# Output projection of a hybrid encoder layer: operands as scaled fp16 pieces, y split where it arises

## The chip, the cores and the metric

The kernel runs on one core of a Trainium2 chip. Each engine (TensorE "PE", VectorE "DVE", ScalarE "ACT", GpSimd "POOL", SyncE "SP") takes its own queue of instructions in order; DMAs are issued from SP's queue. The metric is the device time of one execution in microseconds, the median of the runs. Lower is better.

## The reference

One layer on x of 1024 tokens by 1024 features, in float32. Eight heads of group A attend in a sliding window with ALiBi and learned sinks, eight of group B to their own chunk and eight chunks before it with a learned bias. Each group's output is normalised over its 512 columns with a gain of its own; both together go through one output projection, and the result is added to x. An MLP with squared ReLU follows.

```python
n = rms_norm(x, g)
q, k, v = split(n @ w_in)                       # columns of groups A and B
ya = rms_norm(mixer_a(qa, ka, va, sinks), ga)   # 512 columns
yb = rms_norm(mixer_b(qb, kb, vb, rel_bias), gb)
h = x + concat(ya, yb) @ w_out                  # the part that is changed
out = rms_norm(h + relu(rms_norm(h) @ w1) ** 2 @ w2)
```

## The kernel before

Tokens stand in 8 blocks of 128 (tb), or 2 halves of 512 (t). Heads go in pairs of 128 columns: A0 to A3 are m = 0 to 3, B0 to B3 are m = 4 to 7. Attention runs in units, A0_0 to A3_6 and then B0_0 to B7_1 (a head of B and a half): scores S, softmax rows P, transposes pt copied to T_A (group A; ACT L630, DVE L177) or transposed by DMA to G_B (group B), and products with V in PSUM "av". Between the pieces of a unit, a Filler places steps of the input projections (PSUM ip_qA1, ip_vB3 and so on) and later the steps of the first half of the output projection, out_proj_a (PSUM op_A, tag "w", two banks, which the input projections share). out_proj_b (op_B) follows after the last unit, at the start of the MLP part.

Every large product is made of pieces: mm3 (L200) issues y0*w0, y0*w1 and y1*w0, where index 0 is an operand rounded to a narrower type and 1 what is left of it. In the output projection the pieces are fp32r, 4 bytes each. out_proj_step makes one such triple for a pair q, a token block tb and a half of the columns; 8 blocks by 2 halves by 4 pairs by 3 products are 192 matmuls of 128x512 for each of op_A and op_B.

What makes the operands:

- **y of group A.** UnitA.apply (L800, L801) adds up the two halves of PSUM into Y; Pair.finish (L678 on) stores Y to DRAM (ya, 8 x 256 KB). load_ya brings it back ahead of op_A (four for t = 0, four for t = 1), and split_ya splits it with the norm's gain ogc: a copy on ACT (L914), the rest on DVE (L917). SPLIT_FIRST and SPLIT_AT say in which steps.
- **y of group B.** finish splits Y directly, with the gain and V's scale in one factor (V[2]); m = 4 to 6 go out to yd and come back (load_y, 512 KB a half), m = 7 stays.
- **w_out.** out_weight loads 128 rows into st_o, copies on ACT (L228) and subtracts on POOL (L177, 32 of 128x256).
- **norms.** squares of Y are added up in sqA and sqB; group_rstd turns them with 16 one-column matmuls (ss_A, ss_B) into rows of tokens; ACT (L1064) multiplies op_A by it while it empties PSUM, and residual (L1242) does so for op_B.

The order: matmuls keep the program's order (pe, "program order"). The other engines' queues, SP's among them, are put in order by a scheduler before the run; each engine then waits at the head of its queue. Tiles come from pools with tags: "pg" (33 pages), "ws" (three staging tiles of 4 KB a partition, in which st_kB, st_qB, st_vB and st_o land), "tst". A DMA into a tile can only be issued when its last reader is done.

## Time and profile before

| | us |
|---|---|
| median of 3 runs | 1041.23 (1040.61 to 1041.39) |
| the profiled execution | 1040.53 |
| its span | 1038.7 |
| TensorE busy | 1000.8 |
| op_A, 192 matmuls | 58.0 |
| op_B, 192 matmuls | 46.8 |

The span runs from the first instruction to the last; some 1.8 us of the execution lie around it. "Busy" for matmuls counts overlapping time: a mean duration of 428 or 396 ns (op_A, op_B) is longer than the distance from one start to the next, so the pace is read from unbroken runs in the chain of waits. A row of the timeline has start, duration, engine, line and operation, and in brackets how long the engine was idle before it and what ended that.

### The profile page before, as it was taken

What the parts mean: (1) busy time and instruction counts of PE and PEld (TensorE: products, weight loads), DVE (VectorE), ACT (ScalarE), POOL (GpSimd) and SP (SyncE); (2) the same over time, 40 slices, a digit from 0 to 9 for tenths busy, and PEclk for the clock granted to TensorE, in tenths of its full rate; (3) what the DMA queues carried; (4) which work ended last, traced back from release to release, by engine and by line L of the source; (5) the groups of instructions that cost most, each with busy time, mean ns of one, the idle gap of its engine ahead of it and who ended that gap; (6) DMA issues with size and microseconds to landing.
All of it is one profiled execution on the core that took longest, in us unless ns stands there. A gap on an engine that the chain in (4) does not pass through costs nothing.

```text
span 1038.7 us, 14057 instructions
## 1 busy us (share of the span) xinstructions
PE 1000.8 (96%) x4818; PEld 591.8 (57%) x4818; DVE 742.5 (71%) x1259; ACT 692.6 (67%) x1102; POOL 443.9 (43%) x341
## 2 busy tenths in 40 slices
...
PEclk9999999999989999989999999999999999999999
...
GB/s 353 254 133 133 129 82 184 194 209 225 209 257 251 207 261 182 62 21 166 211 282 293 205 210 274 195 170 310 257 329 388 189 150 186 159 121 122 1 1 162
DMA packets 150567, 200.63 MB, mean 193 GB/s; under 512 B 78688, under 2 KB 96224, under 8 KB 150496
## 3 DMA queue, kind: packets, MB, share of 16 engines
...
q8 instruction: 38, 0.62, 0.3%
...
## 4 chain that ended last, share of the span: by engine, by line
PE 34%; ACT 8%; issue 7%; DMA 7%; DVE 6%; POOL 2%; SPq 1%; DVEq 0%; POOLq 0%; ACTq 0%
PE f_a L171 13%; PE f_c L171 7%; PE f L171 6%; PE f_b L171 4%; DMA w<-in_w_ff_dram 3%; PE op_B L171 2%; ACT w L1362 2%; DMA m<-in_w_ff_dram 2%; DMA u<-ud 2%; POOL W L1397 2%; ACT k L1459 1%; ACT k L1458 1%; ACT W L1395 1%; DMA G_B<-H_B 1%; ACT m L1176 1%
## 5 line engine op out<-in xcount | busy, mean ns | idle before, releaser
L171 PE MATMUL f<-X,W 128*128 128x512 f16 x1344 | 295.3, 381 | 6.6 <-POOL W L1397 5.0
L171 PEld LDWEIGHTS <-U 128*128 128x128 f16 x1356 | 133.0, 98 | 163.9 <-issue 7.2
L171 PEld LDWEIGHTS <-W 128*128 128x128 f16 x1344 | 131.4, 98 | 166.3 <-POOL W L1397 8.2
L1397 POOL TENSOR_TENSOR U<-u,U 128x1024 f16<-128x1024 f32 x48 | 117.3, 2454 | 170.5 <-ACT U L1395 155.2
L171 PE MATMUL f_a<-V,U 128*128 128x512 f16 x756 | 165.3, 379 | 1.0 <-DVE C L1711 1.0
L1397 POOL TENSOR_TENSOR W<-T,W 128x1024 f16<-128x1024 f32 x29 | 69.7, 2407 | 84.3 <-ACT W L1395 84.3
L1397 POOL TENSOR_TENSOR W<-w,W 128x1024 f16<-128x1024 f32 x21 | 51.6, 2458 | 98.6 <-ACT W L1395 98.6
L171 PE MATMUL f_c<-V,U 128*128 128x512 f16 x384 | 86.0, 384 | 3.5 <-DVE V L1399 2.2
L1393 ACT ACTIVATE u<-u,uup 128x1024 f32<-128x1024 f32 x48 | 53.9, 1141 | 53.1 <-DMA u<-ud 53.0
L1399 DVE SCALAR_TENSOR_TENSOR V<-Z,up,V 128x1024 f16<-128x1024 f32 x32 | 51.3, 1605 | 28.7 <-ACT V L1395 20.7
L1395 ACT ACTIVATE U<-u 128x1024 f16<-128x1024 f32 x48 | 50.2, 1046 | 28.1 <-DVE Z L1369 10.4
L623 ACT ACTIVATE P_B<-P_B,nm_B 128x640 f32<-128x640 f32 (+2 forms) x64 | 44.2, 691 | 32.2 <-DVE nm_B L620 16.6
L171 PE MATMUL op_A<-w_o,y 128*128 128x512 f32 x192 | 58.0, 428 | 4.1 <-DVE ts_vB L433 3.9
L868 DVE SCALAR_TENSOR_TENSOR H_B<-P_B,rc_B,H_B 128x640 f16<-128x640 f32 (+2 forms) x64 | 51.0, 825 | 13.6 <-ACT H_B L863 13.3
L1399 DVE SCALAR_TENSOR_TENSOR V<-w,up,V 128x1024 f16<-128x1024 f32 x24 | 42.2, 1756 | 18.0 <-ACT V L1395 13.8
L171 PE MATMUL ip_qB<-nT,w_qB 128*128 128x512 f32 x192 | 53.7, 406 | 1.1 <-DVE t_kB L407 1.0
L171 PE MATMUL ip_kB<-nT,w_kB 128*128 128x512 f32 x192 | 53.7, 405 | 0.0
L1457 DVE CUSTOM_DVE_ANT_0 k<-f,k 128x1024 f32<-128x1024 f32 x24 | 29.3, 1220 | 31.3 <-PE f L171 22.4
L171 PE MATMUL ip_vB<-nT,w_vB 128*128 128x512 f32 x192 | 51.3, 400 | 0.0
L1395 ACT ACTIVATE V<-Z,up 128x1024 f16<-128x1024 f32 x32 | 36.4, 1138 | 22.2 <-DVE Z L1369 19.3
L171 PE MATMUL ip_qA<-nT,w_qA 128*128 128x512 f32 x192 | 50.7, 398 | 0.3 <-DVE VA L177 0.3
L863 ACT ACTIVATE H_B<-P_B,rc_B 128x640 f16<-128x640 f32 (+2 forms) x64 | 40.8, 685 | 9.5 <-DVE rc_B L860 4.2
...
## 6 DMA issues: line engine op xcount, KB each, us to landing
w<-in_w_ff_dram SPq DMA_DIRECT2D x64, 512.0 KB, 7.5
u<-ud SPq DMA_DIRECT2D x56, 512.0 KB, 5.4
ud<-k SPq DMA_DIRECT2D x48, 512.0 KB, 3.1
m<-in_w_ff_dram SPq DMA_DIRECT2D x32, 512.0 KB, 5.8
...
xr<-in_x_dram SPq DMA_DIRECT2D x8, 512.0 KB, 8.8
st_o<-in_w_out_dram SPq DMA_DIRECT2D x8, 512.0 KB, 4.8
h<-in_x_dram SPq DMA_DIRECT2D x8, 512.0 KB, 4.9
```

Source lines behind the costliest of these rows:

```text
L171: pe(nc.tensor.matmul(*args, **kw))
L623: nc.scalar.activation(pr, pr, AF.Exp, bias=nm, scale=-1.0, accum_out=sm)
L863: nc.scalar.activation(hi, q, AF.Copy, scale=rc)
L868: nc.vector.scalar_tensor_tensor(lo, q, rc, hi, ALU.mult, ALU.subtract)
L1176: nc.scalar.activation(src, src, AF.Square, accum_out=self.column())
L1362: nc.scalar.activation(w, w, AF.Copy, scale=up1)
L1393: nc.scalar.activation(full, full, AF.Copy, scale=up)
L1395: nc.scalar.activation(w[0], full, AF.Copy, scale=1.0 if up is None else up)
L1397: engine.tensor_tensor(w[1], full, w[0], ALU.subtract)
L1399: engine.scalar_tensor_tensor(w[1], full, up, w[0], ALU.mult, ALU.subtract)
L1457: dve.tensor_tensor_reduce(v, ps, v, 1.0, 0.0, ALU.add, ALU.max, top)
L1458: nc.scalar.activation(v, v, AF.Relu, scale=down1[n])
```

## The change

- **Scale of group A's y.** While V of group A is made, DVE takes the largest magnitude of each half (topA). scale_of_y turns it into powers of two: upA, by which Y is scaled as it leaves PSUM (ACT's copy and DVE's addition, now a SCALAR_TENSOR_TENSOR), dnA and dnA2, by which the norm undoes it. Group B's V is scaled already; its Y gets 2^-14.
- **Split where it arises.** finish splits every Y into two fp16 pieces (copy on ACT, subtraction on POOL, on DVE for the last one). Pairs 0 to 5 go to yd (two DMAs of 256 KB each) and come back as one of 512 KB; pairs 6 and 7 stay. ya, split_ya, split_y and their places are gone.
- **Weights.** The gain goes into w_out. A power of two per group is taken from a bound of its rows: bound_weights loads each of the eight 128-row blocks once more (bo0 to bo7, staging tag "ws") in the units 2 to 9, and the unit after squares it on ACT with a running sum. scale_of_weights makes the scale per group at B2_0 and at B7_0, each with one 128x128 transpose on TensorE (all_o0, all_o1) and some ten small DVE operations. out_weight then copies with that factor on ACT and takes the rest on DVE; POOL has no part in it any more.
- **Undoing.** rA is multiplied by dnA and owdn, rB by owdn.
- PAD, an unused strip of memory, grows from 32 to 40, and one small tile moves to another pool.

```diff
-SPLIT_FIRST = {(1, 1, 2): 0, (1, 1, 5): 1}
-SPLIT_AT = {(0, 0): (2, 0), (0, 2): (3, 0), (2, 1): (0, 1), (2, 3): (1, 1), (2, 5): (2, 1), (2, 7): (3, 1)}
...
+Y_UP, Y_DOWN, O_UP = 13, 14, 12
+BOUND_AT = 2
+SPREAD_B = "B7_0"
+PAD = 40
...
+    yd = dram([6, P, 2, 2, HALF], "yd", F16)
...
+    def root_of_bits(e):
+        i = e.bitcast(I32)
+        nc.vector.tensor_scalar(i, i, float(1 << 23), 0.5, ALU.add, ALU.mult)
+        nc.vector.tensor_scalar(i, i, 0xFF << 23, None, ALU.bitwise_and)
+        nc.vector.tensor_scalar(i, i, 1.0, float(63 << 23), ALU.mult, ALU.add)
+        return e
...
+    def bits_over(cols, name, psum, tag, bufs, least):
+        top = scale_tile("gtop", name, 2)
+        nc.vector.tensor_reduce(top, cols, mybir.AxisListType.X, ALU.max)
+        spread = psum.tile([P, P], F32, tag=tag, bufs=bufs, name=f"all_{name}")
+        transpose(spread, top.to_broadcast([P, P]), ident)
+        top = scale_tile("gall", name, 2)
+        nc.vector.tensor_reduce(top, spread, mybir.AxisListType.X, ALU.max)
+        return bits_of(top, name, least)
...
             nc.vector.tensor_tensor(f(st[:, 0]), acc, R1[:, c], ALU.mult)
+            nc.vector.tensor_reduce(
+                topA[:, t : t + 1], f(st[:, 0]), mybir.AxisListType.X, ALU.max, apply_absolute_value=True
+            )
...
-                for k, _ in enumerate(in_proj(*a, wa, (t,))):
-                    if (t, i, k) in SPLIT_FIRST:
-                        split_ya(SPLIT_FIRST[t, i, k], 0)
-                    yield
+            for a, wa in zip((q, v), w):
+                yield from in_proj(*a, wa, (t,))
...
-            if self.kind == "A":
-                nc.sync.dma_start(ya[self.m, :, t], Y)
-            elif self.y is None:
-                y = page([P, 2, HALF], f"y{t}_{self.m}")
-                low = split_y(y, Y, self.V[2], by_act)
-                def rest():
-                    if by_act:
-                        low()
-                    nc.sync.dma_start(yd[self.m - 4, :, t], f(y))
-                if by_act:
-                    late.append(rest)
-                else:
-                    rest()
+            if self.y is None:
+                y = page([P, 2, HALF], f"y{t}_{self.m}", F16)
             else:
-                self.y.append(page([P, 2, HALF], f"y{t}_{self.m}"))
-                split_y(self.y[t], Y, self.V[2])
+                if t == 0:
+                    self.y.append(page([P, 2, 2, HALF], f"y_{self.m}", F16))
+                y = self.y[0][:, t]
+            nc.scalar.activation(y[:, 0], Y, AF.Copy)
+            low = nc.vector if (self.m, t) == (7, 1) else nc.gpsimd
+            low.tensor_tensor(y[:, 1], Y, y[:, 0], ALU.subtract)
+            if self.y is None:
+                nc.sync.dma_start(yd[self.m, :, t], y)
...
-                nc.scalar.activation(y, self.av[HD:, :, s, :], AF.Copy)
-                nc.vector.tensor_tensor(y, self.av[:HD, :, s, :], y, ALU.add)
+                nc.scalar.activation(y, self.av[HD:, :, s, :], AF.Copy, scale=upA[HD:])
+                nc.vector.scalar_tensor_tensor(y, self.av[:HD, :, s, :], upA[:HD], y, ALU.mult, ALU.add)
...
+    def scale_of_y():
+        e = bits_over(topA, "yA", aps, "w", 2, -50)
+        power(upA, e, -1.0, 254 + Y_UP)
+        power(dnA, e, 1.0, -Y_UP)
+        nc.vector.tensor_scalar(dnA2, dnA, dnA, 1.0 / HALF, ALU.mult, ALU.mult)
+        nc.vector.tensor_tensor(og2, ogc, ogc, ALU.mult)
+    def scale_of_weights(group):
+        c = slice(4 * group, 4 * group + 4)
+        t = small.tile([P, 4], F32, tag="wbound", bufs=2, name=f"wbound{group}")
+        g = ogc[:, c]
+        if group:
+            g = gains[:, c]
+            nc.vector.tensor_tensor(og2[:, c], g, g, ALU.mult)
+        nc.vector.tensor_tensor(t, wsq[:, c], og2[:, c], ALU.mult)
+        e = root_of_bits(bits_over(t, f"o{group}", aps, "w", 2, -80))
+        up = scale_tile("oup", str(group), 2)
+        power(up, e, -1.0, 254 + O_UP)
+        power(owdn[:, group : group + 1], e, 1.0, -O_UP)
+        nc.vector.tensor_scalar(gains[:, c], g, up, None, ALU.mult)
+    def bound_weights(m):
+        st = stage([P, D], f"bo{m}")
+        load(st, w_out[m * P : (m + 1) * P, :])
+        return lambda: nc.scalar.activation(st, st, AF.Square, accum_out=wsq[:, m : m + 1])
...
-        nc.vector.tensor_scalar(v, ps, 1.0 / HALF, EPS, ALU.mult, ALU.add)
+        nc.vector.tensor_scalar(v, ps, dnA2, epsA, ALU.mult, ALU.add)
...
+        nc.vector.tensor_scalar(r, r, dnA, owdn[:, :1], ALU.mult, ALU.mult)
...
-    def load_y(m, halves=range(2)):
-        y = [page([P, 2, HALF], f"y{t}_{m}") for t in halves]
-        for tile_y, t in zip(y, halves):
-            nc.sync.dma_start(f(tile_y), yd[m - 4, :, t])
+    def load_y(m):
+        y = page([P, 2, 2, HALF], f"y_{m}", F16)
+        nc.sync.dma_start(y, yd[m])
         return y
-    def load_ya(m, t):
-        y = page([P, 2, HALF], f"y{t}_{m}")
-        nc.sync.dma_start(f(y[:, 1]), ya[m, :, t])
-        return y
-    def split_ya(m, t):
-        y = ys_a[m][t]
-        split_y(y, f(y[:, 1]), ogc[:, m : m + 1])
     def out_weight(m):
-        return load_weight(w_out[m * P : (m + 1) * P, :], [P, D], f"o{m}", pool, 1, 2)
-    hres, ys_a = {}, []
+        st = stage([P, D], f"st_o{m}")
+        w = page([P, 2, D], f"w_o{m}", F16)
+        load(st, w_out[m * P : (m + 1) * P, :])
+        g = gains[:, m : m + 1]
+        for j in range(2):
+            c = slice(j * HALF, (j + 1) * HALF)
+            in_turn("o", nc.scalar.activation(w[:, 0, c], st[:, c], AF.Copy, scale=g))
+            nc.vector.scalar_tensor_tensor(w[:, 1, c], st[:, c], g, w[:, 0, c], ALU.mult, ALU.subtract)
+        return w[:, 0], w[:, 1]
...
-        y = ys[q][tb // 4][:, :, tb % 4 * P : (tb % 4 + 1) * P]
+        y = ys[q][:, tb // 4, :, tb % 4 * P : (tb % 4 + 1) * P]
...
-        ys, ws = ys_a, []
-        for m in range(4):
-            ys.append([load_ya(m, 0)])
+        ys, ws = [], []
         for m in range(4):
             ws.append(out_weight(m))
+            ys.append(load_y(m))
...
-            if tb == 1:
-                for m in range(4):
-                    ys[m].append(load_ya(m, 1))
...
+        if n == 2:
+            scale_of_y()
+    bound = None
+    for n, (unit, name, n_fill) in enumerate(units):
+        if bound is not None:
+            bound()
+        bound = bound_weights(n - BOUND_AT) if 0 <= n - BOUND_AT < 8 else None
         if unit.name == "B2_0":
+            scale_of_weights(0)
             rA = group_rstd("A", aps, "w", 2, None)
+        if unit.name == SPREAD_B:
+            scale_of_weights(1)
         ahead.remove(unit)
         if unit is units[-1][0]:
-            for m in (4, 5, 6):
-                ys.append(load_y(m))
+            for m in range(4, 8):
+                ys.append(load_y(m) if m < 6 else y67[m - 6])
...
-    for m in (7,):
-        ys.append(load_y(m) if m < 7 else y7)
-        ws.append(out_weight(m))
+    ys[2:] = [y67[0][0], y67[1][0]]
...
+    nc.vector.tensor_scalar(rB, rB, owdn[:, 1:], None, ALU.mult)
```

How it moves instructions, at three places. First SP's queue in group A, after the copies of K; st_kB0, st_qB0 and st_vB0 are the weights of the input projection of B0, QqA1 the rows of q of A1. Before:

```order
L380 DMA KA3_200<-ts_kA_1_538 64x512 x2
L127 DMA st_kB0_998<-in_w_in_dram 128x1024
L127 DMA st_qB0_1221<-in_w_in_dram 128x1024
L377 DMA QqA10_675<-ts_qA1_0_677 64x512
L377 DMA QqA11_676<-ts_qA1_0_677 64x512
L377 DMA QqA10_675<-ts_qA1_0_677 64x512
L377 DMA QqA11_676<-ts_qA1_0_677 64x512
L377 DMA QqA10_675<-ts_qA1_1_778 64x512
L377 DMA QqA11_676<-ts_qA1_1_778 64x512
L127 DMA st_vB0_1453<-in_w_in_dram 128x1024
```

With the change:

```order
L424 DMA KA3_209<-ts_kA_1_548 64x512 x2
L130 DMA bo0_933<-in_w_out_dram 128x1024
L130 DMA st_kB0_1027<-in_w_in_dram 128x1024
L421 DMA QqA10_686<-ts_qA1_0_688 64x512
L421 DMA QqA11_687<-ts_qA1_0_688 64x512
L421 DMA QqA10_686<-ts_qA1_0_688 64x512
L421 DMA QqA11_687<-ts_qA1_0_688 64x512
L130 DMA bo1_1041<-in_w_out_dram 128x1024
L130 DMA bo2_1139<-in_w_out_dram 128x1024
L421 DMA QqA10_686<-ts_qA1_1_802 64x512
L421 DMA QqA11_687<-ts_qA1_1_802 64x512
L130 DMA bo3_1220<-in_w_out_dram 128x1024
```

Two loads of w_out (bo1, bo2) now stand behind the first four copies of QqA, one (bo0) has taken the place of st_kB0, and st_qB0 has moved back behind bo3.

Second, ACT in the same stretch; P are softmax rows, es the sinks, w0_qA3 the coarse piece of a weight, T_A the copies that the products with V wait for. Before:

```order
L369 ACTIVATE ts_qA1_0_677<-ts_qA1_0_677 128x512
L623 ACTIVATE P_A0_2_1_690,sm_A0_2_657<-P_A0_2_1_690,nm_A0_2_656 128x256
L228 ACTIVATE w0_qA3_787<-st_qA3_786 128x1024
L623 ACTIVATE P_A0_2_1_690,sm_A0_2_657<-P_A0_2_1_690,nm_A0_2_656 128x256
L756 ACTIVATE es_A0_2_699<-nm_A0_2_656,psink_81 128x2
L630 ACTIVATE T_A0_0_0_718<-pt_A0_0_0_717 128x256
L630 ACTIVATE T_A0_0_1_727<-pt_A0_0_1_726 128x512
L623 ACTIVATE P_A0_4_0_738,sm_A0_4_735<-P_A0_4_0_738,nm_A0_4_734 128x256 x2
L756 ACTIVATE es_A0_4_766<-nm_A0_4_734,psink_81 128x2
```

With the change:

```order
L413 ACTIVATE ts_qA1_0_688<-ts_qA1_0_688 128x512
L970 ACTIVATE bo0_933,wsq_184<-bo0_933 128x1024
L231 ACTIVATE w0_qA3_811<-st_qA3_810 128x1024
L663 ACTIVATE P_A0_2_1_714,sm_A0_2_668<-P_A0_2_1_714,nm_A0_2_667 128x256 x2
L789 ACTIVATE es_A0_2_723<-nm_A0_2_667,psink_83 128x2
L670 ACTIVATE T_A0_0_0_742<-pt_A0_0_0_741 128x256
L670 ACTIVATE T_A0_0_1_751<-pt_A0_0_1_750 128x512
L663 ACTIVATE P_A0_4_0_762,sm_A0_4_759<-P_A0_4_0_762,nm_A0_4_758 128x256 x2
L789 ACTIVATE es_A0_4_790<-nm_A0_4_758,psink_83 128x2
L970 ACTIVATE bo1_1041,wsq_184<-bo1_1041 128x1024
L663 ACTIVATE P_A0_4_1_781,sm_A0_4_759<-P_A0_4_1_781,nm_A0_4_758 128x256 x2
L789 ACTIVATE es_A0_4_790<-nm_A0_4_758,psink_83 128x2
```

The Square of bo0 stands ahead of w0_qA3 and T_A0_0_0, the Square of bo1 ahead of P_A0_4_1; bo2 follows three rows further on, directly ahead of T_A0_2_0.

Third, DVE before the second half of V of B3 leaves PSUM (ts_vB3, L433, with the change L477), at 297 to 305 us of the profile before; the bank it empties is the next one of op_A. Before, from the first of the four splits of y on:

```order
L917 SCALAR_TENSOR_TENSOR y0_0_3401<-y0_0_3401,ogc_82 128x512
L405 SCALAR_TENSOR_TENSOR t1_qB3_3317<-ip_qB3_1_3449,R1_180 128x512
L917 SCALAR_TENSOR_TENSOR y0_1_3403<-y0_1_3403,ogc_82 128x512
L917 SCALAR_TENSOR_TENSOR y0_2_3405<-y0_2_3405,ogc_82 128x512
L868 SCALAR_TENSOR_TENSOR H_B5_1_1_3490<-P_B5_1_0_3458,rc_B5_1_3455,H_B5_1_1_3490 128x640
L868 SCALAR_TENSOR_TENSOR H_B5_1_1_3490<-P_B5_1_1_3482,rc_B5_1_3455,H_B5_1_1_3490 128x640
L620 ISA P_B5_1_3_3538,nm_B5_1_3453<-S_B5_1_3_3537,b_B1_587 128x640
L620 ISA nm_B5_1_3453 128x1
L917 SCALAR_TENSOR_TENSOR y0_3_3407<-y0_3_3407,ogc_82 128x512
L908 TENSOR_TENSOR Y6_0_3472<-av_B5_0_3494,Y6_0_3472 64x512
L433 TENSOR_TENSOR ts_vB3_3399<-ip_vB3_1_3548,R1_180 128x512
```

With the change:

```order
L1005 SCALAR_TENSOR_TENSOR w_o2_3508<-st_o2_3507,gains_o_186,w_o2_3508 128x512 x2
L660 ISA P_B5_1_2_3582,nm_B5_1_3529<-S_B5_1_2_3581,b_B1_598 128x640
L660 ISA nm_B5_1_3529 128x1
L449 SCALAR_TENSOR_TENSOR t1_qB3_3407<-ip_qB3_1_3525,R1_189 128x512
L892 TENSOR_SCALAR sm_B5_1_3530<-sm_B5_1_3530 128x2
L893 RECIPROCAL rc_B5_1_3531<-sm_B5_1_3530 128x2
L939 SCALAR_TENSOR_TENSOR Y6_0_3548<-av_B5_0_3570,Y6_0_3548 64x512
L1005 SCALAR_TENSOR_TENSOR w_o3_3517<-st_o3_3516,gains_o_186,w_o3_3517 128x512 x2
L901 SCALAR_TENSOR_TENSOR H_B5_1_1_3566<-P_B5_1_0_3534,rc_B5_1_3531,H_B5_1_1_3566 128x640
L477 TENSOR_TENSOR ts_vB3_3487<-ip_vB3_1_3624,R1_189 128x512
L901 SCALAR_TENSOR_TENSOR H_B5_1_1_3566<-P_B5_1_1_3558,rc_B5_1_3531,H_B5_1_1_3566 128x640
L660 ISA P_B5_1_3_3614,nm_B5_1_3529<-S_B5_1_3_3613,b_B1_598 128x640
```

The four splits of y are gone; splits of w_o2 and w_o3 (those of w_o0 and w_o1 stand a few rows further up) and the rows of P_B5_1 are there in their place, and the second H_B5_1_1 has moved behind ts_vB3.

73 lines of the change are left out of this document (31 added, 42 removed).

## Prediction

> **What bounds the kernel now.** First the page's head: which engine is full, and what the chain that ended last is made of.
>
> ```profile
> span 1038.7 us, 14057 instructions
> PE 1000.8 (96%) x4818; PEld 591.8 (57%) x4818; DVE 742.5 (71%) x1259; ACT 692.6 (67%) x1102; POOL 443.9 (43%) x341
> PEclk9999999999989999989999999999999999999999
> PE 34%; ACT 8%; issue 7%; DMA 7%; DVE 6%; POOL 2%; SPq 1%; DVEq 0%; POOLq 0%; ACTq 0%
> ```
>
> TensorE is busy 96% of the span, so work taken from POOL, VectorE or ScalarE pays only where TensorE waits for it. Only three things can move the end: the pace of the matmuls, TensorE's waits, and the slices in which the granted clock dips. So the second view is the busy time by stretches of 26 us (columns: PE, PEld, DVE, ACT, POOL, PEclk, DMA share, GB/s).
>
> ```profile
> 52.00:78.00 26.00, 24.75 (x139) 20.51 (x138) 18.09 (x57) 18.16 (x52) 15.14 (x17) 1.00 0.50 133
> 78.00:104.00 26.00, 26.00 (x147) 22.27 (x146) 17.79 (x56) 17.06 (x52) 17.44 (x20) 1.00 0.45 132
> 104.00:130.00 26.00, 26.00 (x149) 22.10 (x148) 20.72 (x62) 18.55 (x55) 17.81 (x20) 1.00 0.49 130
> 286.00:312.00 26.00, 20.35 (x90) 15.52 (x89) 20.81 (x44) 19.23 (x36) 15.04 (x21) 0.87 1.05 259
> 416.00:442.00 26.00, 21.49 (x109) 13.95 (x107) 24.34 (x42) 17.80 (x26) 3.35 (x3) 0.97 0.15 61
> ```
>
> From 78 to 130 TensorE doesn't wait at all; there a wait that the change adds is paid in full. At 286 to 312 it loses 5.7 us of waiting, and 0.13 x 26 = 3.4 us more to the clock; there a wait that goes is worth most. At 416 to 442 VectorE is the limit.
>
> **The matmuls of the output projection.** The third view is the chain of waits, in which unbroken runs give the pace (start, us, what, count).
>
> ```profile
> 371.08 1.39 PE op_A L171 x6
> 374.45 8.45 PE op_B L171 x36
> 384.58 8.34 PE op_B L171 x36
> 803.47 20.72 PE f_a L171 x96
> ```
>
> Six op_A in 1.39 and 36 op_B in 8.34 us are both 0.232 us each, with fp32 operands; 96 f_a, whose pieces are fp16, take 0.216 each. The shapes are the same (128x512), as are the three products per step.
>
> ```profile
> L171 PE MATMUL op_A<-w_o,y 128*128 128x512 f32 x192 | 58.0, 428 | 4.1 <-DVE ts_vB L433 3.9
> L171 PE MATMUL op_B<-w_o,y 128*128 128x512 f32 x192 | 46.8, 396 | 0.2 <-ACT o L1064 0.2
> ```
>
> 192 + 192 of them at 0.016 less is 6.1 us. In the last third of op_B VectorE is the limit (24.34 of 26 us above), and what TensorE gains there it waits for; I take 5.3, with ends 4.3 and 6.1.
>
> **The stall at 301 us.** Next the timeline of TensorE and VectorE there.
>
> ```profile
> 300.82 0.40 PE L171 MATMUL S_B<-KkB,QqB 128*128 128x256 f32 x2
> 305.13 1.22 PE L171 MATMUL op_A<-w_o,y 128*128 128x512 f32 x2 [3.92 <-DVE ts_vB L433]
> ...
> 297.34 1.02 DVE L917 SCALAR_TENSOR_TENSOR y<-y,ogc 128x512 fp32r<-128x512 f32 x1 [1.40 <-ACT y L914]
> 298.88 1.40 DVE L917 SCALAR_TENSOR_TENSOR y<-y,ogc 128x512 fp32r<-128x512 f32 x2
> 302.54 0.84 DVE L917 SCALAR_TENSOR_TENSOR y<-y,ogc 128x512 fp32r<-128x512 f32 x1
> 304.38 0.69 DVE L433 TENSOR_TENSOR ts_vB<-ip_vB,R 128x512 f32<-128x512 f32 x1
> ```
>
> op_A wants the PSUM bank that ts_vB empties, and ts_vB stands in VectorE's queue behind four splits of y, which cost 1.40 of waiting and 3.26 of work. The change removes these four. But in the new order w_o0 to w_o3, two splits each, stand at the same place, and the last pair (w_o3) one H_B ahead of it; the nearest duration is that of the splits removed.
>
> ```profile
> L917 DVE SCALAR_TENSOR_TENSOR y<-y,ogc 128x512 fp32r<-128x512 f32 x8 | 7.5, 958 | 3.1 <-ACT y L914 3.1
> DMA to landing us min/median/max: 4.0/4.8/6.3
> ```
>
> Eight at 0.69 (the ts_vB row, same shape) to 0.96 are 5.5 to 7.7 us against 4.66 removed, spread over some 15 us, though; and the second row (st_o, issue to landing) says that w_o3, whose load stands behind those of y, can still come late. So the stall may stay as it is, or go with the clock's 3.4 us: 0 to 7.3. Nothing in the rows lies nearer to one end; I take the middle, 3.7.
>
> **The stall that is added: group A.** The bounds of w_out's rows need eight loads of 512 KB (bo0 to bo7) and eight Squares on ScalarE. In the old order st_kB0, in the new bo0, is what SP issues after the KA copies.
>
> ```profile
> 50.49 1.19 SPq L127 DMA_DIRECT2D st_kB<-in_w_in_dram  x1
> 61.87 0.54 SPq L127 DMA_DIRECT2D st_vB<-in_w_in_dram  x1
> ...
> st_kB<-in_w_in_dram SPq DMA_DIRECT2D x1, 512.0 KB, 4.5
> st_vB<-in_w_in_dram SPq DMA_DIRECT2D x1, 512.0 KB, 3.5
> ...
> 53.69 1.06 ACT L228 ACTIVATE w_qA<-st_qA 128x1024 fp32r<-128x1024 f32 x1 [3.22 <-DMA KA<-ts_kA]
> 55.05 0.19 ACT L623 ACTIVATION_READ_ACCUMULATOR P_A<-P_A,nm_A 128x1 f32 x1
> 55.33 0.85 ACT L630 ACTIVATE T_A<-pt_A 128x256 fp32r<-128x256 f32 x2
> 62.47 1.09 ACT L630 ACTIVATE T_A<-pt_A 128x512 fp32r<-128x512 f32 x2
> ...
> 55.74 0.84 PE L171 MATMUL av_A<-T_A,VA 128*128 128x256 f32 x2 [1.17 <-ACT T_A L630]
> ...
> L335 ACT ACTIVATE xr<-xr 128x1024 f32<-128x1024 f32 x8 | 8.4, 1056 | 0.7 <-DMA xr<-in_x_dram 0.5
> ```
>
> The last row is a Square of the same shape with a running sum: 1.06, plus 0.19 to read the sum, 1.25 us. ScalarE takes its queue in order, and Square(bo0) now stands ahead of w_qA3, that ahead of T_A0_0, for which TensorE already waits 1.17. bo0 lands at 50.49 + 4.5 = 55.0; the Square ends at 56.2, w_qA3 at 57.3, and with two more P_A of some 0.65 each ahead, T_A0_0 starts at 58.6 instead of 55.33: 3.3 us, with nothing to hide them. By the addresses the program gives, bo0, bo1 and bo2 share one of the three staging tiles, so each load can go out only after the Square before. bo1 is issued at 56.2, lands at 60.5 and is squared at 61.4 to 62.6, after T_A0_0 and its neighbours; bo2 is issued at 62.6 and lands 3.5 to 4.5 later, at 66.1 to 67.1; its Square stands directly ahead of T_A0_2, which then starts at 67.3 to 68.4 instead of 62.47: 4.8 to 5.9 in all, not on top of the 3.3. Behind Square(bo2) wait T_A0_2, then the next softmax rows, and through them TensorE. Later Squares stand 7.5 us apart with loads issued ahead, and ScalarE has some 8 of 26 us free (17.06 and 18.55 above), into which Squares and the eight copies of y (0.7 us each) go: absorbed, for the most part. Laying the chain out to T_A0_6 by these durations, its lateness less its slack grows to at most 7.8. The low end is bo0 alone with its Square, 55.0 + 1.25 - 53.69 = 2.6. I take 5.0.
>
> The row of 286 to 312 shows what a stall of 3.92 does to the clock (0.87), that of 52 to 78 that 1.17 does nothing (1.00). A stall of 1.17 + 3.3 = 4.5 at 54 would be of the first kind; at half clock until 65 TensorE would lose up to 3.4, but it then waits for T_A0_2 anyway, so I count it in the upper end (11.2) and not in the sum. The Trainium skill, TensorE: Matmul & The Clock Gate, section What's actually happening, has the clock halve after an idle window of about 3.4 us whose grid doesn't follow the kernel. By that rule the 4.5 us would nearly always halve it, and the sum would be up to 3.4 higher; the trace agrees with it at 301, and only chance decides how the grid falls at 54.
>
> **Smaller places.** At B2_0 the transpose all_o0 and ten small VectorE instructions come in ahead of ss_A.
>
> ```profile
> 223.59 1.90 PE L171 MATMUL ss_A<-ones,sqA 128*128 128x1 f32 x16
> 225.00 0.68 DVE L405 SCALAR_TENSOR_TENSOR t_qB<-ip_qB,R 128x512 f32<-128x512 f32 x1
> 226.62 0.17 DVE L929 TENSOR_SCALAR vgA<-ss_A 128x8 f32<-128x8 f32 x1
> ```
>
> Both PSUM banks "w" are now used there, so ss_A waits for t_qB, which ends at 225.7; the small instructions cost some 0.17 each. Between 0 and 2.1 (223.59 to 225.7); the matmuls of ip_qB can't pass, but t_qB would be less late without anything ahead: 0.7. At the end of attention the copy of w_o7 now stands ahead of o7_1, for which op_B_0 waits.
>
> ```profile
> 368.55 0.37 SPq L127 DMA_DIRECT2D st_o<-in_w_out_dram  x1
> 373.71 0.69 ACT L1064 ACTIVATE o<-op_A,rgA 128x512 f32<-128x512 f32 x1 [2.12 <-PE op_A L171]
> ```
>
> st_o7 lands 4.0 to 6.3 after 368.55 and two copies of 0.62 to 0.7 follow: ready 373.8 to 376.2 against 373.71. Some of it is spared because SP issues one load less ahead of it: 0 to 2.5, taken 0.4.
>
> POOL loses 32 subtractions of w_o and gets 15 of 128x512; VectorE loses 16 splits of y and gets 16 of w_o: no wait of TensorE other than that at 301 ends on either. The bytes of y and w_out through the queue stay at some 14.6 MB. From 450 us on the program is the same; it moves as a whole, at nothing.
>
> **Sum.** Against the profiled execution, 1040.5: -5.3 (matmuls) -3.7 (301) +5.0 (group A) +0.7 +0.4 = 1037.6. That execution was 0.7 below the median of the runs (1041.2), so 1038.3.
>
> **Rivals.** (1) Slower: the loads of bo hold ScalarE through group A. Lateness of 7.8 and half clock of 3.4: 6.2 more than I count, 1044.5. For it: the queue order, no slack at T_A0_0 and T_A0_2, and TensorE that never waits from 78 to 130. Against: ScalarE's free third. It decides from a loss of 10.0 in group A on (5.0 + the 2.9 gained + 0.2%, 2.1). 0.22. (2) No change: at 301 only the releaser changes, from y's splits to w_o's: 1038.3 + 3.7 = 1042.0. For it: as much VectorE work ahead of ts_vB, the last just before it; against: the loads behind it start earlier. 0.25. (3) Much faster: the stall at 301 goes with its slow clock (3.6 more) and group A costs the low end (2.4 less) and the small places nothing: 1031.2. 0.15. (4) The change doesn't do what it says: fp16 weights for TensorE at the old pace of 0.232 us, 1038.3 + 5.3 = 1043.6. Against it stand the f_a, at 0.216 in the same form. 0.03.
>
> **How the numbers follow.** My forecast has 0.35. About 0.2% (2.1 us) is what a measurement of this kernel can tell from no change. Faster: forecast and (3), 0.50; same: (2), 0.25; slower: (1) and (4), 0.25. The range goes from a little below (3), where both large unknowns fall well, 1030, to 1047, which holds (1) with most of the upper ends of the small places (1.4 and 2.1 more).
>
> **What would show it.** The chain should show op_A and op_B at 0.216 in unbroken runs. In group A, av_A of unit A0_0 should wait some 4.5 us for T_A and ScalarE should wait for a DMA into bo; if neither shows, the 5.0 is wrong. At 301 the wait of op_A should be shorter; if it ends on ts_vB after 4 us again, (2) holds. After 450 us stage times should be equal; a dip of the clock that comes or goes there would spoil the sum by 1.7 to 3.4. The forecast fails above all if ScalarE's lateness in group A isn't absorbed after A0_4.

## The result, and the profile after

The changed kernel takes 1058.7 us (median of 4 runs, 1056.75 to 1060.3) against 1041.3 for the kernel before: 1.0166 times the time, 95% interval 1.0150 to 1.0182. It is slower by 17.4 us, where 1038.3 was forecast. One run of the kernel before, beside the later experiments, took 1276.0 us at a mean granted clock of 0.752 and is left out of every ratio. The profiled execution took 1060.3. Its page: span, busy time of each engine, and the shares of the chain that ended last:

```profile
span 1058.5 us, 14063 instructions
PE 1004.1 (95%) x4821; PEld 566.8 (54%) x4821; DVE 758.4 (72%) x1296; ACT 704.4 (67%) x1118; POOL 432.2 (41%) x324
...
PE 35%; ACT 9%; DVE 9%; issue 5%; DMA 4%; POOL 2%; SPq 0%; DVEq 0%; ACTq 0%; POOLq 0%
```

TensorE is busy for 1004.1 us (1000.8 before) in a span 19.8 us longer. What it waits for, the largest rows outside the MLP part (engine, line, what it waited for, us in total, times, longest):

```profile
PE S_B L174 <- DVE nm_B L662: 6.8, 2, 5.4
PE av_A L174 <- ACT T_A L670: 5.2, 2, 3.5
PE S_B L174 <- DVE nm_B L660: 3.6, 3, 1.5
PE op_A L174 <- DVE ts_vB L477: 3.4, 1, 3.4
PE av_A L174 <- DVE T_A L180: 2.0, 3, 0.9
PE ip_kB L174 <- POOL w_kB L180: 1.3, 1, 1.3
PE ss_A L174 <- DVE t_qB L449: 1.3, 1, 1.3
```

Two rows are about as before: op_A (3.9 there) and the S_B that wait for L660 (3.7, then L620). The S_B that wait for L662 were at 1.4, the av_A at 1.2 and 0.3; ip_kB and ss_A didn't wait. In the MLP part the largest differences are f_c's waits for V, 3.4 and 2.0 against 2.2 and 1.2. The stretches of 26 us show a second loss, the granted clock (the column after the brackets of POOL):

```profile
52.00:78.00 26.00, 21.77 (x115) 18.11 (x114) 15.56 (x49) 20.52 (x55) 13.12 (x14) 0.93 0.70 205
78.00:104.00 26.00, 23.97 (x125) 19.84 (x124) 16.41 (x49) 20.49 (x52) 14.46 (x16) 0.93 0.53 155
130.00:156.00 26.00, 23.96 (x135) 20.05 (x134) 19.70 (x60) 17.48 (x48) 21.57 (x24) 1.00 0.39 104
156.00:182.00 26.00, 23.93 (x123) 19.96 (x123) 17.96 (x49) 17.47 (x45) 17.09 (x18) 0.94 0.39 99
234.00:260.00 26.00, 24.72 (x128) 19.58 (x128) 17.19 (x44) 15.44 (x27) 12.02 (x26) 0.93 0.86 196
312.00:338.00 26.00, 22.60 (x108) 13.27 (x107) 19.18 (x46) 16.88 (x33) 3.97 (x5) 0.93 0.98 240
338.00:364.00 26.00, 20.57 (x104) 11.16 (x103) 12.67 (x31) 14.35 (x31) 13.05 (x12) 0.93 0.87 195
```

Five of the seven stand at 0.93, that is 1.8 us less clock each (0.07 x 26), and one at 0.94. Over the whole span the mean granted clock is 0.982 against 0.990: 1058.5 x 0.018 = 19.1 us not granted against 1038.7 x 0.010 = 10.4. So up to some 8.7 us of the loss pass through the clock, all of them if TensorE had work through each of these dips.

TensorE's order is the same in both kernels but for the transposes that were added. So the loss can be placed by the **lateness**: the start of a matmul in one trace less the start of the same matmul in the first trace of the kernel before. Between two columns it grows by what is lost there. The columns are times of the kernel before.

| us, lateness at | 50 | 82 | 140 | 158 | 176 | 222 | 232 | 298 | 318 | 330 | 445 | 760 | 1030 |
|---|---|---|---|---|---|---|---|---|---|---|---|---|---|
| after | 0.6 | 8.9 | 8.8 | 13.3 | 13.6 | 13.6 | 16.8 | 18.0 | 16.0 | 22.5 | 14.8 | 19.6 | 19.6 |
| e1_no_bound | 0.1 | -0.6 | 0.3 | 3.4 | 4.9 | 4.9 | 8.1 | 8.6 | 5.7 | 13.8 | 5.6 | 8.4 | 8.4 |
| e2_y_rest_on_vector | 0.4 | 6.1 | 6.2 | 6.9 | 10.7 | 13.8 | 16.2 | 16.9 | 15.7 | 22.3 | 14.8 | 18.8 | 18.7 |
| e3_bias_early | -0.6 | 6.4 | 6.5 | 12.5 | 12.4 | 12.4 | 15.6 | 17.1 | 14.9 | 16.2 | 10.4 | 15.2 | 15.2 |
| e4_before_late | 1.0 | 0.3 | 0.2 | 0.2 | 0.2 | 0.2 | 0.2 | 0.0 | -0.4 | -0.1 | 4.5 | 9.2 | 9.1 |
| e5_bo_in_pages | 0.6 | 0.7 | 6.6 | 9.3 | 11.2 | 11.3 | 15.8 | 16.4 | 14.5 | 21.6 | 14.1 | 16.1 | 16.3 |
| e6_one_bank | 0.8 | 12.3 | 12.5 | 16.9 | 17.3 | 17.3 | 20.7 | 21.9 | 20.0 | 28.3 | 19.5 | 23.3 | 23.3 |
| e7_mlp_order | 0.0 | 7.3 | 7.8 | 13.9 | 13.9 | 13.9 | 17.0 | 18.1 | 15.6 | 22.8 | 15.0 | 17.2 | 17.2 |
| e8_all_put_right | 0.1 | 3.7 | 8.0 | 10.0 | 15.0 | 18.0 | 21.0 | 21.5 | 19.0 | 21.7 | 13.6 | 17.2 | 17.2 |
| e9_early_spread | 0.2 | 7.5 | 7.4 | 11.9 | 12.3 | 13.6 | 13.6 | 14.7 | 13.5 | 19.9 | 12.2 | 14.4 | 14.4 |
| e10_no_bound_three | 0.2 | -0.8 | -0.2 | 3.1 | 4.5 | 5.9 | 5.9 | 7.0 | 4.0 | 4.6 | -1.1 | 3.3 | 3.3 |
| e11_y21_on_vector | 0.0 | -0.4 | 0.4 | 4.0 | 3.9 | 5.7 | 5.7 | 6.9 | 4.7 | 6.0 | -0.2 | 1.7 | 1.7 |
| e12_bound_spread | 1.3 | 1.2 | 3.7 | 7.0 | 12.9 | 16.5 | 16.5 | 22.1 | 20.5 | 21.2 | 13.6 | 17.7 | 17.7 |
| e13_y20_on_vector | -0.2 | -1.2 | -0.9 | 0.2 | 2.1 | 3.4 | 3.4 | 4.7 | 2.2 | 5.8 | -1.1 | -0.6 | -0.6 |
| e14_late_pinned | 0.9 | 0.3 | 0.1 | 0.1 | 0.2 | 0.2 | 0.2 | 0.0 | -0.3 | 0.2 | 4.5 | 9.2 | 9.2 |
| e15_before_again | 0.5 | -0.1 | -0.2 | -0.2 | -0.2 | -0.2 | -0.2 | -0.2 | 0.9 | 0.9 | 1.3 | 4.2 | 4.2 |

The row "after" has five places of loss: 50 to 82 (8.3 us), 140 to 158 (4.5), 222 to 232 (3.2), 318 to 330 (6.5) and 445 to 760 (4.8). Between 330 and 445 it gains 7.7, at 298 to 318 another 2.0. The experiments take the places one by one. The same place differs by 1 to 3 us between most traces with the same orders, and by 6 in the worst case (at 82: 8.9, 7.3, 7.5, 6.4, 12.3); the dips of the granted clock differ with it (52 to 78: 0.87 in the trace with 12.3, 0.93 in that with 8.9).

### The profile page after: what moved, and what is told of

The parts are those of the page before. It is cut to its first block, busy times and chain, and to the rows that moved or that the text cites. A ratio compares the mean times of both kernels' runs of the same rounds, so it can differ in the third digit from the quotient of the medians.

```text
span 1058.5 us, 14063 instructions
## 1 busy us (share of the span) xinstructions
PE 1004.1 (95%) x4821; PEld 566.8 (54%) x4821; DVE 758.4 (72%) x1296; ACT 704.4 (67%) x1118; POOL 432.2 (41%) x324
## 4 chain that ended last, share of the span: by engine, by line
PE 35%; ACT 9%; DVE 9%; issue 5%; DMA 4%; POOL 2%; SPq 0%; DVEq 0%; ACTq 0%; POOLq 0%
PE f_a L174 13%; PE f L174 8%; PE f_c L174 7%; PE f_b L174 4%; PE op_B L174 2%; POOL W L1428 2%; DMA u<-ud 2%; ACT w L1393 1%; DVE T L1400 1%; DMA m<-in_w_ff_dram 1%; ACT W L1426 1%; DVE X L1316 1%; ACT k L1490 1%; DVE tops_w L1208 1%; ACT k L1489 1%
## 5 line engine op out<-in xcount | busy, mean ns | idle before, releaser
L901 DVE SCALAR_TENSOR_TENSOR H_B<-P_B,rc_B,H_B 128x640 f16<-128x640 f32 (+2 forms) x64 | 51.3, 823 | 14.3 <-ACT H_B L896 13.9
L174 PEld LDWEIGHTS <-y 128*128 128x128 f16 x384 | 36.6, 100 | 41.8 <-DVE ts_vB L477 3.6
L1430 DVE SCALAR_TENSOR_TENSOR V<-w,up,V 128x1024 f16<-128x1024 f32 x24 | 42.5, 1771 | 19.7 <-ACT V L1426 15.6
L174 PE MATMUL op_A<-w_o,y 128*128 128x512 f16 x192 | 51.5, 395 | 3.4 <-DVE ts_vB L477 3.4
L174 PE MATMUL S_B<-KkB,QqB 128*128 128x320 f32 (+2 forms) x192 | 44.1, 339 | 10.4 <-DVE nm_B L662 6.8
L1426 ACT ACTIVATE V<-Z,up 128x1024 f16<-128x1024 f32 x32 | 36.5, 1139 | 21.6 <-DVE Z L1400 19.4
```

The costliest lines, as they stand in the source:

```text
L174: pe(nc.tensor.matmul(*args, **kw))
L901: nc.vector.scalar_tensor_tensor(lo, q, rc, hi, ALU.mult, ALU.subtract)
L1426: nc.scalar.activation(w[0], full, AF.Copy, scale=1.0 if up is None else up)
L1430: engine.scalar_tensor_tensor(w[1], full, up, w[0], ALU.mult, ALU.subtract)
```

## The experiments

Most times below are medians of two runs (e15 has 1, e4 3, e8 4, e12 5, e10 and e11 8, e13 10), and the changed kernel itself ran from 1056.75 to 1060.3. A time that differs by 2 us from its 1058.7 doesn't show a gain by itself; the lateness in one trace shows where something changed.

**Group A, and what holds ScalarE.** ScalarE's timeline of the changed kernel (in brackets the idle time before the row and what ended it):

```profile
55.07 1.06 ACT L970 ACTIVATE bo<-bo 128x1024 f32<-128x1024 f32 x1 [5.59 <-DMA bo<-in_w_out_dram]
58.24 0.84 ACT L670 ACTIVATE T_A<-pt_A 128x256 fp32r<-128x256 f32 x2
...
64.86 1.06 ACT L970 ACTIVATE bo<-bo 128x1024 f32<-128x1024 f32 x1 [0.29 <-DMA bo<-in_w_out_dram]
66.04 0.60 ACT L670 ACTIVATE T_A<-pt_A 128x512 fp32r<-128x512 f32 x1
...
81.14 1.06 ACT L970 ACTIVATE bo<-bo 128x1024 f32<-128x1024 f32 x1 [2.69 <-DMA bo<-in_w_out_dram]
85.09 0.60 ACT L670 ACTIVATE T_A<-pt_A 128x512 fp32r<-128x512 f32 x1
```

T_A, which TensorE waits for, stands behind a Square that stands behind a load: at 55 and again at 81. The first experiment takes loads and Squares out.

```diff
-        st = stage([P, D], f"bo{m}")
-        load(st, w_out[m * P : (m + 1) * P, :])
-        return lambda: nc.scalar.activation(st, st, AF.Square, accum_out=wsq[:, m : m + 1])
+        return lambda: None
...
+    nc.vector.memset(wsq, 1.0)
```

> The changed kernel without the eight loads of w_out's rows and the eight Squares in group A (their sums are a constant, so the bound of the weights is left out). Theory A, that ScalarE waits in group A for these loads and works on these Squares: the lateness of the matmuls against the kernel before, 8.9 us at unit A0_6 with the changed kernel, falls below 1.5 there, and the time falls by 8 to 11, to about 1049. Rival B, that the scaled copies of Y and the pieces of y made in group A hold it up: lateness at A0_6 stays above 5 and the time above 1055.

1049.4 us (2 runs), 9.3 less, and no lateness at 82 or 140 us. Theory A holds; scaled copies and pieces of y cost nothing before 140. Next the loads go into tiles of the page pool, Squares unchanged:

```diff
-        st = stage([P, D], f"bo{m}")
+        st = page([P, D], f"bo{m}", F32)
```

> The changed kernel with the eight loads bo in tiles of the page pool instead of the three staging tiles; all Squares are kept. If ScalarE's loss in group A is waiting (each load could go out only after the Square before), the lateness at unit A0_6 (8.9 us with the changed kernel, 6.1 and 6.4 in two runs with the same orders there, -0.6 without loads and Squares) falls to 3 or less. If it is the work of the Squares, it stays at 5 or more.

At 82 us lateness is 0.7, as expected if it was the waiting. But this doesn't decide it: in the new order the first Square runs at 79 us, so only one had run by then, where the changed kernel had run six. The lateness comes at 102 us, and the time is 1057.9:

```profile
100.37 1.06 ACT L970 ACTIVATE bo<-bo 128x1024 f32<-128x1024 f32 x1 [1.83 <-DMA bo<-in_w_out_dram]
102.62 1.06 ACT L970 ACTIVATE bo<-bo 128x1024 f32<-128x1024 f32 x1 [0.60 <-DMA bo<-in_w_out_dram]
103.79 0.60 ACT L670 ACTIVATE T_A<-pt_A 128x512 fp32r<-128x512 f32 x1
```

Two Squares in a row, each behind its load, stand again ahead of T_A. So the staging tiles aren't what makes the wait. The changed kernel's own trace parts waiting and work. Its lateness grows from 0.6 to 4.9 around the Square at 55 us and from 4.9 to 8.9 around that at 81, the two that waited long for their load (5.59 and 2.69). The Squares at 69, 74, 94 and 98 us found their load landed, and around them it stands still (4.9, then 8.9 to 8.8). So it was the waiting, and the clock behind it.

**140 to 158 us.** GpSimd's timeline there, changed kernel:

```profile
151.32 0.98 POOL L794 TENSOR_SCALAR P_A<-P_A,rc_A 128x256 f32<-128x256 f32 x1 [1.73 <-ACT y L727]
152.28 1.15 POOL L729 TENSOR_TENSOR y<-Y,y 128x512 f16<-128x512 f32 x1
153.41 0.92 POOL L794 TENSOR_SCALAR P_A<-P_A,rc_A 128x256 f32<-128x256 f32 x1
154.29 2.78 POOL L180 TENSOR_TENSOR w_kB<-st_kB,w_kB 128x256 fp32r<-128x256 f32 x4
```

In the kernel before, w_kB1's row stood ahead of these two rows of P_A:

```profile
143.17 2.83 POOL L177 TENSOR_TENSOR w_kB<-st_kB,w_kB 128x256 fp32r<-128x256 f32 x4 [4.01 <-PE ip_vB L171]
```

Now w_kB1, which ip_kB waits for, stands behind the rest of y (L729) and behind two rows of P_A that the change doesn't name. Of the 4.5 us, ip_kB's waits for w_kB1 are 2.0 (0.70 for ScalarE's piece, 1.34 for GpSimd's) and one of av_A for T_A is 0.9 (0.3 in the kernel before); the remaining 1.9 fall together with the granted clock of 0.94 in 156 to 182. All of group A's rests of y on VectorE:

```diff
-            low = nc.vector if (self.m, t) == (7, 1) else nc.gpsimd
+            low = nc.vector if (self.m, t) == (7, 1) or self.kind == "A" else nc.gpsimd
```

> The changed kernel with the rest of y (the second piece) made on VectorE instead of GpSimd for group A. Theory C, that GpSimd's extra subtractions make w_kB1 late at 143 to 157 us (lateness grows from 8.9 to 13.7 there): growth between unit A1_2 and A3_4 falls to 2 or less and the time by 2 to 4. Rival D, that this wait has another cause (w_kB1's load or ScalarE) or goes over to VectorE: growth stays above 3.5, time within 2 of 1058.7.

Growth at 140 to 158 falls from 4.5 to 0.7, but 3.8 come at 158 to 176, where ip_qB now waits 3.2 us for VectorE (t_kB, 1.0 in the kernel before); up to 176 it is 4.5 against 4.8, and the time is 1057.7. Theory C is right about the place, rival D about the time: the wait goes over to VectorE.

**222 to 232 us.** VectorE's timeline, and then TensorE's, of the changed kernel:

```profile
238.02 0.68 DVE L449 SCALAR_TENSOR_TENSOR t_qB<-ip_qB,R 128x512 f32<-128x512 f32 x1
```

```profile
238.75 1.95 PE L174 MATMUL ss_A<-ones,sqA 128*128 128x1 f32 x16 [1.28 <-DVE t_qB L449]
```

ss_A takes its bank from a pool of two; all_o0, which the change adds ahead of it, has one, and the other comes free when t_qB has read ip_qB. The first try puts all_o0 and ss_A in one bank (all_o0 in its first 128 columns, ss_A in the next eight):

```diff
-        ps = psum.tile([P, TB], F32, tag=tag, bufs=bufs, name=f"ss_{kind}")
+        ps = one_bank["o0"][:, P : P + TB] if kind == "A" else psum.tile([P, TB], F32, tag=tag, bufs=bufs, name=f"ss_{kind}")
```

> The changed kernel with all_o0 and ss_A in one PSUM bank, so that ss_A needs no second one. If the growth of 3.2 us at 222 to 232 us (in three runs) is ss_A's wait for the bank that t_qB empties, with the half clock after it, it falls below 1. If it is the small instructions on VectorE ahead of the softmax rows, it stays above 2.

Growth stays at 3.4 (1061.3 us), and it doesn't decide: ss_A now waits 1.5 us for the reduction of all_o0, which stands behind the same t_qB in VectorE's queue. The second makes the scale three units earlier:

```diff
-        if unit.name == "B2_0":
+        if unit.name == "B1_0":
             scale_of_weights(0)
+        if unit.name == "B2_0":
             rA = group_rstd("A", aps, "w", 2, None)
```

> The changed kernel with the scale of the first four weights (all_o0 and its small instructions) made three units earlier, at B1_0. If the growth of 3.2 us at 222 to 232 us comes from ss_A waiting behind t_qB because all_o0 has taken the other place, it falls below 1 there, and less than 1 appears at B1_0 (about 190 us), since no second tile is wanted there. If it is merely moved, 2 or more appear there.

No growth at 222 to 232, 1.3 between 176 and 222 (between the two marks, less than 1 and 2 or more), 1056.4 us. So it was the place of all_o0; of the 3.2, 1.3 is the wait, and the lower clock behind it (0.93 in 234 to 260 above) fits the rest. All traces bear that out: in the eight in which the sixteen matmuls of ss_A wait, 0.57 to 1.51 us, the granted clock in 226 to 252 is 0.87 to 0.93; in the other nine, in which they don't wait, it is 1.00.

**318 to 330 us.** VectorE waits here for the bias of the last head, masked on GpSimd after its load; SP's queue in the changed kernel shows why it is late, and VectorE's timeline (second) what waits:

```profile
335.31 4.12 SPq L904 DMA_TRANSPOSE G_B<-H_B  x1
339.48 0.57 SPq L703 DMA_DIRECT2D b_B<-in_relb_dram  x1
```

```profile
343.26 0.29 DVE L662 CUSTOM_DVE_ANT_0 P_B<-S_B,b_B 128x128 f32<-128x128 f32 x1 [5.20 <-POOL b_B L707]
```

The scheduler has moved this load from two rows behind the first transposes of H_B5_1 to behind the last of them. In the kernel before it went out here:

```profile
307.10 0.54 SPq L663 DMA_DIRECT2D b_B<-in_relb_dram  x1
```

The edit gives that bias a tile of its own and loads it with the one before:

```diff
+            if (self.j, s) == (3, 1):
+                return
             nc.sync.dma_start(bias_b[s], relb[2 * self.j + s])
             self.bias.append(bias_b[s])
+            if self.j == 3:
+                self.bias.append(page([P, 5 * P], "b_B1p", F32))
+                nc.sync.dma_start(self.bias[1], relb[7])
```

> The changed kernel with the bias of the last head in a tile of its own, so that its load stands eleven places further up in SP's queue. Theory E, that the wait of 5.6 us at 338 us is the load of that bias, issued at 339.5 behind the transposes: the wait falls below 1, lateness does not grow there (15.7 to 22.8 now), the time falls by 5 to 7, to about 1052.5. Rival F, that PE would wait there for GpSimd's h or for the rows of P anyway: less than 2.5 gained.

Growth there is 1.3 instead of 6.5, and S_B's wait is gone (av_B waits 1.8 for a transpose instead): the load was the cause. The time falls by 2.1 only, to 1056.6, where 5 to 7 was expected; by the time alone rival F would have had it. Of the 5.2 won here, 1.9 are given back up to 445 us, where this trace gains 5.8 and the changed kernel's 7.7. That leaves 3.3, and the rest lies within what traces with the same orders differ by.

**After 445 us.** The kernel before, with more matmuls ahead of that stretch:

```diff
             opb[tb] = pair_psum(f"op_B_{tb}")
+            for _ in range(16 if tb == 0 else 0):
+                matmul(opb[tb][:, 0], ys[0][0][:, 0, :P], ws[0][0][:, :HALF], start=True, stop=True)
```

> The kernel before with 16 more matmuls (3.7 us) at the start of the second half of the output projection, results thrown away; nothing else is changed. Theory G, that the stretch after 450 us moves as a whole: the time grows by what is left of the 3.7 at 440 us, and lateness stays constant within 1 us from 450 us to the end. Rival H, that the stretch isn't rigid (waits of TensorE fall differently into the windows of the clock): lateness changes by 2 or more between 450 us and the end, up or down.

The added matmuls (16 of 0.232 us) make the lateness 4.5 at 445 us, but it grows to 9.2: a later start costs more than itself here (1049.8 us in all against 1040.9). VectorE's order has two swaps in both this kernel and the changed one: k0_1 ahead of S1_1 near 470 us, and C000 ahead of V0_5 near 750. In the changed kernel:

```profile
766.67 1.28 DVE L1743 SCALAR_TENSOR_TENSOR C<-f_a,down,C 128x1024 f32<-128x1024 f32 x1
767.86 1.27 DVE L1430 SCALAR_TENSOR_TENSOR V<-Z,up,V 128x1024 f16<-128x1024 f32 x1
```

V, which f_c waits for, stands behind C; in the kernel before it stands two rows ahead of it:

```profile
748.71 1.28 DVE L1399 SCALAR_TENSOR_TENSOR V<-Z,up,V 128x1024 f16<-128x1024 f32 x1
749.90 1.28 DVE L1399 SCALAR_TENSOR_TENSOR U<-u,uup,U 128x1024 f16<-128x1024 f32 x1
751.10 1.28 DVE L1711 SCALAR_TENSOR_TENSOR C<-f_a,down,C 128x1024 f32<-128x1024 f32 x1
```

The swaps are put back by a dependence without a wait in the schedule:

```diff
+            pin(engine.scalar_tensor_tensor(w[1], full, up, w[0], ALU.mult, ALU.subtract), name)
...
+        pin(ins, None, "U1_5")
...
+            pin(ins, None, "S1_1" if (n, p) == (0, 2) else None)
```

> The changed kernel with two places of VectorE's order in the MLP put back to that of the kernel before (S1_1 ahead of k0_1 near 470 us, C000 behind U1_5 near 750 us). If lateness grows there by 4.8 us (445 to 760 us) because the scheduler has swapped these rows, growth falls to 2 or less, and to 0.5 or less between 745 and 760 (2.4 now), and the time by 3 to 4. If the clock's grid or the loads do it, growth stays above 3.5.

> The kernel before with 16 more matmuls at 374 us, and with S1_1 ahead of k0_1 and C000 behind U1_5 as in the kernel before. Without these two the lateness grew from 4.5 at 445 to 9.2 at 760. If the swapped rows are the cause, growth is 1.5 or less. If the stretch is bound by other engines' chains and by the clock, it is 2.5 or more.

> The kernel before, unchanged, for a second trace. Lateness against the first trace stays within 1 us at every place if executions are alike; 2 or more after 445 us would say that this stretch differs by itself.

In the changed kernel growth from 445 to 760 falls from 4.8 to 2.2 (1056.9 us), but it is still 2.4 at 745 to 760; expected were 2 or less, 0.5 or less, and 3 to 4 us of time. In the kernel before with 16 more matmuls it stays at 4.7 (1048.6). And the kernel before, unchanged, in its second trace grows by 2.9 from 445 us on (1044.8; other runs 1039.0 to 1045.9). Two stretches of this second trace:

```profile
624.00:650.00 26.00, 24.44 (x106) 10.81 (x107) 19.83 (x17) 15.11 (x18) 17.16 (x7) 0.93 0.85 275
754.00:780.00 26.00, 26.00 (x111) 11.24 (x110) 26.00 (x17) 18.31 (x19) 13.82 (x6) 0.91 0.99 311
```

The same two in the first trace of the kernel before:

```profile
624.00:650.00 26.00, 26.00 (x122) 11.91 (x121) 20.18 (x18) 15.10 (x20) 14.63 (x6) 1.00 0.81 265
754.00:780.00 26.00, 26.00 (x121) 11.68 (x120) 26.00 (x17) 21.56 (x22) 15.55 (x6) 0.99 1.01 328
```

The program is the same, but the granted clock is 0.93 and 0.91 in the one and 1.00 and 0.99 in the other. So up to 2.9 of the 4.8 are what this stretch differs by itself; the first trace, from which I worked, is somewhat fast (13 of the kernel's 49 other runs were faster). The swaps explain less. The first costs 1.0 in the changed kernel, at 470 to 475 us, where f waits for topf; with it put back the growth there is 0.0 (2.0 and 0.0 in e4 and e14). The second costs nothing in all: put back, f_c waits 2.23 instead of 3.42 for VectorE's V, but 3.08 instead of 2.03 for ScalarE's. And the growth at 745 to 760, 2.4 in the changed kernel with and without the swap, is 2.0 in the unchanged kernel's second trace. In the other runs with the swaps put back the stretch grows by 4.4, 1.9, 4.1 and 0.5. What decides between these beyond the clock stays open.

**Together.** All five edits at once:

> All five edits together: bo in pages, y's rest of group A on VectorE, the last bias early, one bank for all_o0 and ss_A, the two places in the MLP put back. If the causes add up (about 6 + 3 + 4 + 2.5 + 3 us), the time is 1038 to 1042, level with the kernel before or a little faster, with the faster matmuls (7 us in 318 to 445) showing. If they hide each other, it stays above 1046.

1056.6 us (1054.8 to 1063.1), 1.0151 [1.0108, 1.0194]: the single gains don't add up. The bias stretch grows by 2.7 and the MLP by 3.6, less than without the edits, but by 222 us lateness is 18.0, more than with no edit (13.6). By the table, 3.0 of that come at 176 to 222, where the rests of y on VectorE cost 3.1 alone (e2) and the Squares in pages 0.1 (e5). Up to 176 both put work before TensorE's operands, and which of them costs what was not taken apart. The same places without the bound, with the last bias early, the scale early and the two swaps put back:

> Without the eight loads and Squares (the bound of the weights is left out), with the last bias early, the scale of the weights early, and the two places in the MLP put back. Growth by place should add up: none in group A up to 140 us, about 4.6 at 140 to 176 (untouched), none at 222 to 232, 1.5 instead of 8 at 318 to 330, 2 after 445: 1049.4 - 3 - 5 - 1 = 1040 to 1041. If they hide each other as in the run with all five, 1045 or more.

1042.75 us, 1.0013 [0.9993, 1.0032]: without the Squares the gains add up to within 2 us of what was expected (1040 to 1041); growth after 445 us is 4.4 where 2 was expected. Then, on top of that, y's rest of pair A2 on VectorE, once the second half and once the first:

```diff
-            low = nc.vector if (self.m, t) == (7, 1) else nc.gpsimd
+            low = nc.vector if (self.m, t) in ((7, 1), (2, 1)) else nc.gpsimd
...
+            low = nc.vector if (self.m, t) in ((7, 1), (2, 0)) else nc.gpsimd
```

> As the run before it in this list, with the rest of one half of y (pair A2, second half) on VectorE, the one that stands in GpSimd's queue ahead of w_kB1 and there waits for ScalarE's copy. If that one wait makes the 3.1 us at 140 to 158, growth falls below 1 there; growth of 1 to 1.5 at 158 to 176 stays. Time 1037 to 1039. If other rows hold w_kB1, no change.

> As the run without the bound and with three places put right (1042.75), with the rest of the first half of pair A2's y on VectorE: the row that stands in GpSimd's queue two places ahead of w_kB1. If its wait for ScalarE's copy, and that copy ahead of ScalarE's w_kB1, make the growth of 3.1 to 3.6 us at 140 to 158, it falls to 1.5 or less (ScalarE's copy stays). If not, it stays at 3. Time 1039 to 1041 against 1042 to 1043.

The second half was the wrong one: no gain, 1043.4, growth 3.6. The first half is the row ahead of w_kB1: growth falls from 3.3 to 1.1, and the time to 1039.95, 0.9996 [0.9982, 1.0009]; the two intervals overlap. The reason isn't quite the expected one: the wait of 1.71 us that ends with ScalarE's copy of y is still there on GpSimd, now ahead of two rows of P_A. What is gone is the row of 1.15 us for y, and with it 0.6 of ip_kB's wait (1.35 to 0.74). The rest of the 2.2 falls together with the granted clock, 1.00 in 130 to 156 instead of 0.93. Last, e10 with the bound again, its loads in pages and spread over the units:

```diff
-        return lambda: None
+        st = page([P, D], f"bo{m}", F32)
+        load(st, w_out[m * P : (m + 1) * P, :])
+        return lambda: nc.scalar.activation(st, st, AF.Square, accum_out=wsq[:, m : m + 1])
...
-        bound = bound_weights(n - BOUND_AT) if 0 <= n - BOUND_AT < 8 else None
+        bound = bound_weights(n // 3 - 1) if n % 3 == 0 and 0 < n // 3 < 9 else None
```

> A complete kernel: the eight loads and Squares in page tiles and spread over units 3 to 24 (every third), the last bias early, the scale early, the MLP's two places put back. If ScalarE's loss in group A comes from the Squares standing close together and waiting for loads, lateness at 140 us falls from 8.8 to 3 or less, and the time to 1042 to 1046. If each Square costs its own wait wherever it stands, lateness by 300 us is above 12 and the time above 1050.

1053.3 us, 1.0111 [1.0090, 1.0132]: little lateness at 140 (3.7), 22.1 at 298 against 7.0 without the bound (e10); the traced execution is a long one, 1058.4. Spread out, the Squares cost about what they cost together: 10.5 us by the medians (1053.3 - 1042.75), where taking them out of the changed kernel had won 9.3. The trace shows why: the loads now go out only 3.5 to 6 us before their Squares, and ScalarE waits for seven of the eight, 15.5 us in all (8.7 for four in the changed kernel). The best version with the bound, this one, is 12.3 us slower than the kernel before; without the bound the new output projection is level with the old one. A version in which all eight loads have landed before their Squares was not run.

## Why the prediction was wrong

- **The pace of the matmuls** was right. The chain of waits of the changed kernel:

```profile
388.47 1.29 PE op_A L174 x6
401.28 10.38 PE op_B L174 x48
```

  Both are 0.215 to 0.216 us a matmul, as f_a's were. 330 to 445 us gains 7.7; the forecast of 5.3 was for the pace alone. 315 of the 384 matmuls lie there, 5.0 us at 0.016 each; where the other 2.7 come from isn't shown.
- **The stall at 301 us**: the wait is 3.40 instead of 3.92, and the row 312 to 338 has 0.93 where 286 to 312 had 0.87. 2.0 us gained where 3.7 was taken, within its ends. The mechanism was rival (2)'s: ts_vB now stands behind the split of w_o3, which itself waits for ScalarE's copy of that weight.

```profile
322.54 2.28 PE L174 MATMUL op_A<-w_o,y 128*128 128x512 f16 x6 [3.40 <-DVE ts_vB L477]
...
318.65 1.42 DVE L1005 SCALAR_TENSOR_TENSOR w_o<-st_o,gains_o,w_o 128x512 f16<-128x512 f32 x2 [2.57 <-ACT w_o L1004]
321.80 0.68 DVE L477 TENSOR_TENSOR ts_vB<-ip_vB,R 128x512 f32<-128x512 f32 x1
```

- **Group A** was right in mechanism and too small: 8.3 to 8.9 against 5.0, in a range of 2.6 to 11.2. bo0's Square (55.07) and T_A0_0 (58.24 for a forecast 58.6) came as worked out. What failed is "absorbed, for the most part": at 81 us ScalarE waited another 2.69 us for a load and TensorE behind it. And the slow clock, which I kept in the upper end since TensorE "then waits for T_A0_2 anyway", came twice (0.93 in both stretches); TensorE had no wait for T_A0_2.
- **The smaller places**: all_o0 cost 3.2, not 0.7: its 1.3 us of waiting has a lower clock behind it. The wait for o7_1 is 0.2 as before, where 0.4 more was taken.
- **The step that failed most** is the sentence that GpSimd's and VectorE's exchange of work ends in no wait of TensorE but the one at 301, and the search for new waits at the edits alone. GpSimd has less work in all, yet its queue is in order: w_kB1 stands behind two rows of P_A and the rest of y, and ip_kB waits 2.0 us for it (4.5 us of lateness there, with the clock and a wait for T_A). A load that the change doesn't touch, the last bias, was moved by the scheduler behind SP's transposes; S_B waits 5.4 us on VectorE for it (6.5 of lateness). The sum had both at nothing.
- **"After 450 us the program is the same; it moves as a whole"**: 4.8 us, where the sum had nothing. Two rows are swapped, of which one costs 1.0, and the stretch differs by some 3 us between two executions of the same kernel, with the granted clock.

Rival (1), ScalarE held through group A, names a loss that is there, but it doesn't decide: its mark was a loss of 10.0, and 8.3 to 8.9 instead of 5.0 would have made some 1042, level with the kernel before. Even its 1044.5 had only one of five places. In the two profiled executions the forecast was 1037.6 and the time 1060.3. The 22.7 between them are, by the table: group A 3.9 more than counted, w_kB1 4.5, all_o0 2.5 more, 1.2 between 232 and 298 (its cause is open), 1.7 less won at 301, the bias 6.5, the MLP 4.8, and 2.4 more won in 330 to 445. By the medians the miss is 20.4; the first trace was faster than its kernel's median by 0.7, the changed kernel's slower by 1.6.
